# A hybrid attention block on one core: the stick-breaking scan reads its sigmoid from PSUM, and one PSUM bank moves from the transposed weights to the scores

## The chip, the cores and the metric

The kernel runs on one core of a Trainium2 chip. The metric is the device time of one execution in microseconds (us). Before the change the median of three runs is 3167.59 us (3167.34 to 3170.79).

## What is computed

The program is one layer of a streaming encoder on 2048 positions of width 1024, all in float32: a projection of the normalised input into the queries, keys and values of two attention groups (differential attention with 4 heads, stick-breaking attention with 8 heads), an output projection, a feed-forward part, and a last normalisation. The change lies in the stick-breaking group:

```
def stick_breaking(q, k, v, norm_g):
    # beta = sigmoid(q.k/sqrt(d)); A[t,s] = beta[t,s] * prod_{s<j<t} (1 - beta[t,j]), s < t
    ...
        z = jnp.einsum('bqhd,bkhd->bhqk', qb, kb) * scale
        ...
        suffix = lax.cumsum(neg_log_1m_beta, axis=3, reverse=True)
        log_a = jax.nn.log_sigmoid(z) - (suffix - neg_log_1m_beta)
        a = jnp.where(mask, jnp.exp(log_a), 0.0)
        outs.append(jnp.einsum('bhqk,bkhd->bqhd', a, v[:, :t1].astype(jnp.float32)))
```

The weight of a key is its beta times the product of (1 - beta) of all later keys. The kernel forms that product with a scan that runs backwards along the keys, with 1 - beta = sigmoid(-z).

## The kernel before

The sequence is cut into four tiles of 512 positions (T = 0 to 3). A tile has eight units g: 0 to 3 are the differential heads, 4 to 7 hold two stick-breaking heads each. The first half of the program (up to about 1500 us) is attention. Beside the attention of one unit, the projection of the next one (`project`, three matmuls of fp32r halves, lines 314 to 316) is issued in small pieces, and in the last unit the output projection of tile 0. The order is a written-out list of steps: `scores_of` of a stage is issued up to `LA_S = 3` stages ahead of `weigh_of`, and a scheduler with priorities then fixes the queue of each engine when the program is built. Which PSUM bank a tile gets is fixed there too.

PSUM has eight banks: two for projections (pool `ps_p`), two for scores (`ps_s`, `PSS = 2`), three for transposed things (`ps_t`, `PST = 3`), one for outputs (`ps_o`). A stick-breaking stage is a pair j of query blocks, a head m and a chunk c of 512 keys. For each of its two query blocks, here called a row of work:

- TensorE (PE) writes the scores to a bank of `ps_s` (lines 668, 669, on the diagonal also 671).
- ScalarE (ACT) reads them twice: sigmoid(-z) to the tile half `om` (line 830) and sigmoid(z) to `be` (831). Both lie in the SBUF tile `row`. Behind them it copies one carried column (836).
- VectorE (DVE) scans `om` backwards in place (834). Both data operands of this instruction are the same SBUF tile.
- GpSimd (POOL) multiplies `be` by the shifted `om` (837, on the diagonal 839).

`weigh` then takes up to four 128x128 blocks: PE transposes them into a bank of `ps_t` (691, tile `ps_at`), ACT copies them to SBUF (696 for head m = 0, 700 otherwise), for m = 0 DVE also forms the rest `al` (697, it reads the same bank), and two or three groups later PE multiplies by the values (715 and 716, or 723). The differential heads use the same two pools: DVE reads their scores (777), ACT takes the exponential (782), and their transposed weights go through 691 and 700.

`transpose_v` (line 644) uses `ps_t` too: the values of the next unit are transposed into a bank (649, tile `ps_vt`), which ACT (655, 656, or 651) and DVE (657) empty as soon as a slot of the value pool is free.

Of the kernel before, what the change touches and what calls it, by code (L numbers as in the profile page):

```python
# [13 lines left out]
AF = mybir.ActivationFunctionType  # L14
ALU = mybir.AluOpType
# [47 lines left out]
FIN = 6  # L63
KB = 5
VB = 5
PSS = 2
PST = 3
PSO = 1
PSP = 2
ROWB = 5  # L70
# [27 lines left out]
def hybrid_block(ctx, tc, xT, n1g, w_in, lq1, lk1, lq2, lk2, subg, sbg, w_out, n2g, w_up, w_down, fg, outT):  # L98
    nc = tc.nc
    PE, V, A, G = nc.tensor, nc.vector, nc.scalar, nc.gpsimd  # L100
# [217 lines left out]
    def blk(d):  # L318
        return slice(d * P, (d + 1) * P)
# [4 lines left out]
    def defer(fn, steps):  # L324
        later.append([steps, fn])
# [98 lines left out]
    with ExitStack() as pa:  # L424
# [6 lines left out]
        ap_ = pa.enter_context(tc.tile_pool(name="ap", bufs=2))  # L431
        ps_s = pa.enter_context(tc.tile_pool(name="ps_s", bufs=PSS, space=PSUM))
        ps_t = pa.enter_context(tc.tile_pool(name="ps_t", bufs=PST, space=PSUM))
        ps_o = pa.enter_context(tc.tile_pool(name="ps_o", bufs=PSO, space=PSUM))
# [228 lines left out]
        def scores(T, g, m, qb, c, n, diag):  # L663

            kv = kt[T, g, c]
            q2, ql = q2t[T, g], qlt[T, g]
            ps = ps_s.tile([P, TW], F32, tag="ps", name="ps_sc")
            PE.matmul(ps[:, :n], lhsT=q2[:, m, blk(qb)], rhs=kv[:, m * TW:m * TW + n], start=True, stop=False)  # L668
            PE.matmul(ps[:, :n], lhsT=ql[:, m, blk(qb)], rhs=kv[:, m * TW:m * TW + n], start=False, stop=not diag)  # L669
            if diag:  # L670
                PE.matmul(ps[:, n - P:n], lhsT=identb, rhs=maskb, start=False, stop=True)
            return ps
# [62 lines left out]
        def finish(T, g, j, po):  # L735

            ot = ap_.tile([P, 2 * P], F32, tag="ot", name="ot")
            A.copy(ot, po)
            nc.sync.dma_start(o_scr[T][g][:, j * 256:(j + 1) * 256], ot)
            sq = ap_.tile([P, 2 * P], F32, tag="osq", name="osq", bufs=1)  # L740
            A.activation(out=sq, in_=ot, func=AF.Square, scale=lam_inv8 if g < NDIFF else 0.125)
            nh, h0 = (1, g) if g < NDIFF else (2, 4 + 2 * (g - 4))
            out = mean_sq[T % 2].rearrange("p (h b) -> p b h", h=NHEADS)[:, 2 * j:2 * j + 2, h0:h0 + nh]
            V.reduce_sum(out=out, in_=sq.rearrange("p (b h c) -> p b h c", h=nh, c=P // nh), axis=mybir.AxisListType.X)
            if g == NG - 1 and j == 1:
                head_rms(T)

        def next_po():
            return ps_o.tile([P, 2 * P], F32, tag="po", name="po")
# [61 lines left out]
        def sb_stages(T, g):  # L811
            out = []
            state = {}

            def stage(j, m, c):
                last_kb = 4 * T + 2 * j + 1
                mine = {}

                def scores_of():
                    row = rowp.tile([P, 2052], F32, tag="row", name="row")  # L820
                    tv = row.rearrange("p (q k c) -> p q k c", q=2, k=2)
                    prev = state.get((j, m))
                    state[j, m] = tv
                    mine["tv"] = tv
                    for qq in range(2):
                        qb = 2 * j + qq
                        n = TW if c < T else (qb + 1) * P
                        ps = scores(T, g, m, qb, c, n, c == T)
                        be, om = tv[:, qq, 0, :], tv[:, qq, 1, :]
                        A.activation(out=om[:, :n], in_=ps[:, :n], func=AF.Sigmoid, scale=-1.0)  # L830
                        A.activation(out=be[:, :n], in_=ps[:, :n], func=AF.Sigmoid)
                        rev = om[:, :n][:, ::-1]
                        init = 1.0 if c == T else prev[:, qq, 1, 0:1]
                        V.tensor_tensor_scan(out=rev, data0=rev, data1=rev, initial=init, op0=ALU.mult, op1=ALU.bypass)  # L834
                        if c < T:
                            A.copy(om[:, n:n + 1], prev[:, qq, 1, 0:1])
                            G.tensor_tensor(out=be[:, :n], in0=be[:, :n], in1=om[:, 1:n + 1], op=ALU.mult)  # L837
                        else:
                            G.tensor_tensor(out=be[:, :n - 1], in0=be[:, :n - 1], in1=om[:, 1:n], op=ALU.mult)
                        yield  # L840

                def weigh_of():
                    tv = mine["tv"]
                    hi_kb = last_kb if c == T else 4 * c + 3

                    def done():
                        if c > 0:
                            return
                        if m == 1:
                            finish(T, g, j, state[j, 1, "po"]["po"])  # L850
                            return

                        oq = ap_.tile([P, 2 * P], F32, tag="oq", name="oq")
                        A.copy(oq, mine_po["po"])  # L854
                        po = state.setdefault((j, 1, "po"), {})

                        def join():
                            if "po" not in po:
                                po["po"] = next_po()
                            for qq in range(2):  # L860
                                PE.matmul(po["po"][:, qq * P:qq * P + 64], lhsT=oq[:, blk(qq)], rhs=fold,
                                          start="open" not in po, stop=False)
                                po["open"] = True

                        def late_join():
                            if "fold" in po:
                                po.pop("fold")()

                        po["fold"] = join
                        defer(late_join, FIN)  # L870

                    mine_po = state.setdefault((j, m, "po"), {})
                    yield from weigh(T, g, mine_po, list(range(4 * c, hi_kb + 1)),
                                     lambda qq, kb: tv[:, qq, 0, blk(kb - 4 * c)], False, m, last_kb, c == T, c == 0, done)

                return scores_of, weigh_of, 2, 2 * (j + 1) if c == T else 4

            return [stage(j, m, c) for j in range(2) for m in range(2) for c in range(T, -1, -1)]
# [317 lines left out]
```

## Time and profile before

| | |
|---|---|
| median of 3 runs | 3167.59 us |
| the profiled execution | 3167.63 us |
| its span in the trace | 3165.6 us |
| mean granted clock of TensorE | 0.981 |
| PE busy | 3002.9 us (95%) |
| DVE busy | 1806.9 us (57%) |
| ACT busy | 1230.7 us (39%) |
| POOL busy | 1054.8 us (33%) |

The span is the time between the first and the last instruction of the trace; the execution is 2.0 us longer. Busy time is the union of an engine's instructions. The ends of matmuls are modelled, so short gaps of PE can be larger than they look. [...]

### The profile page before, as it was taken

What the parts mean: (1) busy time and instruction counts of PE and PEld (TensorE: products, weight loads), DVE (VectorE), ACT (ScalarE), POOL (GpSimd) and SP (SyncE); (2) the same over time, 40 slices, a digit from 0 to 9 for tenths busy, and PEclk for the clock granted to TensorE, in tenths of its full rate; (3) what the DMA queues carried; (4) which work ended last, traced back from release to release, by engine and by line L of the source; (5) the groups of instructions that cost most, each with busy time, mean ns of one, the idle gap of its engine ahead of it and who ended that gap; (6) DMA issues with size and microseconds to landing.
All of it is one profiled execution on the core that took longest, in us unless ns stands there. A gap on an engine that the chain in (4) does not pass through costs nothing.

```text
span 3165.6 us, 42061 instructions
## 1 busy us (share of the span) xinstructions
PE 3002.9 (95%) x15562; PEld 2512.8 (79%) x15562; DVE 1806.9 (57%) x2841; ACT 1230.7 (39%) x2414; POOL 1054.8 (33%) x733
## 2 busy tenths in 40 slices
PE   7888999999989999988988999999999999999997
PEld 5677887888878888877776888888887788888886
DVE  5465567665777767889545444444446544444445
ACT  5344566645766547767333111111113111111113
POOL 3353034202453003556333323332235333333234
PEclk9999999999999999999999999999999999999998
DMA  7777655555443543331666111111114311111111
GB/s 250 253 242 237 210 186 186 162 168 174 137 150 111 154 135 111 114 101 32 212 204 204 48 46 54 47 53 47 40 54 137 103 53 54 47 47 52 42 47 54
DMA packets 153277, 376.73 MB, mean 119 GB/s; under 512 B 20336, under 2 KB 35184, under 8 KB 153072
## 3 DMA queue, kind: packets, MB, share of 16 engines
q1 hardware_dynamic: 153072, 374.04, 37.0%
q8 instruction: 123, 2.02, 0.3%
q14 instruction: 82, 0.67, 0.1%
HBM read 261.24 MB, written 70.78 MB: 105 GB/s over the span
## 4 chain that ended last, share of the span: by engine, by line
PE 45%; DVE 2%; DMA 2%; issue 1%; ACT 1%; POOL 0%; SPq 0%; DVEq 0%; POOLq 0%; ACTq 0%
PE ps_d L314 7%; PE ps_u L315 7%; PE ps_d L315 7%; PE ps_u L316 7%; PE ps_d L316 7%; PE ps_u L314 7%; DMA om<-os 1%; PE ps_h L314 1%; PE ps_h L316 1%; PE ps_h L315 1%; DMA xr<-in_xT 1%; POOL sqs L1035 0%; DVE acc L1056 0%; DVE sqs L394 0%; DMA hraw<-hs 0%
## 5 line engine op out<-in xcount | busy, mean ns | idle before, releaser
L834 DVE TENSOR_TENSOR_SCAN row<-row 128x512 f32<-128x512 f32 (+2 forms) x320 | 429.2, 1351 | 128.1 <-ACT row L830 109.9
L1109 DVE TENSOR_TENSOR acc<-ps_d,acc 128x512 f32<-128x512 f32 (+1 forms) x520 | 348.5, 680 | 253.4 <-PE ps_d L316 252.7
L314 PE MATMUL ps_d<-uh,dh 128*128 128x512 f32 (+1 forms) x1040 | 403.2, 388 | 2.6 <-DVE acc L1109 2.6
L315 PE MATMUL ps_d<-ul,dh 128*128 128x512 f32 (+1 forms) x1040 | 402.8, 387 | 0.0
L316 PE MATMUL ps_d<-uh,dl 128*128 128x512 f32 (+1 forms) x1040 | 402.3, 387 | 0.0
L254 POOL TENSOR_TENSOR wl<-wr,wh 128x1024 fp32r<-128x1024 f32 x119 | 289.6, 2434 | 249.1 <-ACT wh L230 221.1
L314 PE MATMUL ps_proj<-xh,wh 128*128 128x512 f32 x768 | 334.7, 436 | 10.0 <-ACT xh L530 6.9
L837 POOL TENSOR_TENSOR row<-row 128x512 f32<-128x512 f32 x192 | 248.4, 1301 | 255.8 <-DVE row L834 156.9
L254 POOL TENSOR_TENSOR dl<-wr,dh 128x1024 fp32r<-128x1024 f32 x64 | 152.0, 2395 | 542.0 <-ACT dh L230 542.0
L315 PE MATMUL ps_proj<-xl,wh 128*128 128x512 f32 x768 | 309.7, 403 | 14.4 <-POOL xl L525 12.9
L316 PE MATMUL ps_proj<-xh,wl 128*128 128x512 f32 x768 | 310.0, 404 | 9.4 <-POOL wl L254 8.8
L723 PEld LDWEIGHTS po<-v,at 128*128 128x128 f32 x2176 | 286.3, 194 | 28.7 <-ACT oq L854 8.4
L723 PE MATMUL po<-v,at 128*128 128x128 f32 (+1 forms) x2176 | 293.9, 276 | 6.4 <-ACT oq L854 5.1
L691 PE MATMUL ps_at<-ident,row 128*128 128x128 f32 x1632 | 259.1, 276 | 27.6 <-DVE al L697 20.1
L1096 DVE TENSOR_TENSOR ul<-u,uh 128x512 fp32r<-128x512 f32 x128 | 179.1, 1399 | 180.1 <-ACT uh L1095 180.0
L230 ACT CAST dh<-wr 128x1024 fp32r<-128x1024 f32 x64 | 64.1, 1049 | 553.1 <-PE ps_d L315 553.1
L668 PE MATMUL ps_sc<-k,q 128*128 128x512 f32 (+3 forms) x640 | 257.9, 404 | 19.8 <-DMA q<-pjh 10.3
L1092 POOL TENSOR_TENSOR u<-u 128x512 f32<-128x512 f32 x128 | 134.4, 1050 | 395.2 <-DVE u L1091 381.2
L1091 DVE SCALAR_TENSOR_TENSOR u<-ps_u,rb 128x512 f32<-128x512 f32 x128 | 88.4, 691 | 300.4 <-PE ps_u L316 300.4
L691 PEld LDWEIGHTS ps_at<-ident,row 128*128 128x128 f32 x1632 | 197.7, 144 | 63.9 <-issue 14.9
L1095 ACT CAST uh<-u 128x512 fp32r<-128x512 f32 x128 | 79.7, 622 | 414.6 <-POOL u L1092 414.6
L669 PE MATMUL ps_sc<-k,qlow 128*128 128x512 f32 (+3 forms) x640 | 234.1, 367 | 0.0
(184 smaller groups left out, 6307.0 us busy)
## 6 DMA issues: line engine op xcount, KB each, us to landing
wh<-ws SPq DMA_DIRECT2D x72, 512.0 KB, 3.6
wl<-ws SPq DMA_DIRECT2D x72, 512.0 KB, 4.4
wr<-in_w_up SPq DMA_DIRECT2D x64, 512.0 KB, 3.7
wr<-in_w_down SPq DMA_DIRECT2D x64, 512.0 KB, 3.5
k<-ks SPq DMA_DIRECT2D x48, 512.0 KB, 4.3
q<-pjh SPq DMA_DIRECT2D x128, 128.0 KB, 3.1
wr<-in_w_out SPq DMA_DIRECT2D x32, 512.0 KB, 4.9
ws<-wh SPq DMA_DIRECT2D x24, 512.0 KB, 5.0
```

The costliest lines, as they stand in the source:

```text
L254: G.tensor_tensor(out=wl, in0=wr, in1=f32(wh), op=ALU.subtract)
L314: PE.matmul(ps, lhsT=wh[:, cs], rhs=xh, start=start, stop=False)
L315: PE.matmul(ps, lhsT=wh[:, cs], rhs=xl, start=False, stop=False)
L316: PE.matmul(ps, lhsT=wl[:, cs], rhs=xh, start=False, stop=stop)
L668: PE.matmul(ps[:, :n], lhsT=q2[:, m, blk(qb)], rhs=kv[:, m * TW:m * TW + n], start=True, stop=False)
L669: PE.matmul(ps[:, :n], lhsT=ql[:, m, blk(qb)], rhs=kv[:, m * TW:m * TW + n], start=False, stop=not diag)
L691: PE.transpose(pt[:, o:o + P], getter(qq, kb), ident)
L723: PE.matmul(po["po"][:, qq * P + c0:(qq + 1) * P], lhsT=f32(at)[:, so + n * P:so + (n + 1) * P], rhs=vv, start="open" not in po, stop=ends ...
L834: V.tensor_tensor_scan(out=rev, data0=rev, data1=rev, initial=init, op0=ALU.mult, op1=ALU.bypass)
L837: G.tensor_tensor(out=be[:, :n], in0=be[:, :n], in1=om[:, 1:n + 1], op=ALU.mult)
L1096: V.tensor_tensor(out=ul, in0=u, in1=f32(uh), op=ALU.subtract)
L1109: V.tensor_tensor(out=a, in0=ps[:, cs], in1=a, op=ALU.add)
```

## The change

`PSS` and `PST` change places in size: three score banks, two for transposed things. In a stick-breaking row the two sigmoids change their order: sigmoid(z) to `be` comes first, then sigmoid(-z) is written over the scores in their own PSUM bank. The scan reads its first operand from that bank, its second operand, which `bypass` ignores, is `be` in SBUF, and it writes `om` in SBUF as before.

```
-PSS = 2
-PST = 3
+PSS = 3
+PST = 2
...
                         be, om = tv[:, qq, 0, :], tv[:, qq, 1, :]
-                        A.activation(out=om[:, :n], in_=ps[:, :n], func=AF.Sigmoid, scale=-1.0)
                         A.activation(out=be[:, :n], in_=ps[:, :n], func=AF.Sigmoid)
-                        rev = om[:, :n][:, ::-1]
+                        A.activation(out=ps[:, :n], in_=ps[:, :n], func=AF.Sigmoid, scale=-1.0)
+                        rev, src = om[:, :n][:, ::-1], ps[:, :n][:, ::-1]
                         init = 1.0 if c == T else prev[:, qq, 1, 0:1]
-                        V.tensor_tensor_scan(out=rev, data0=rev, data1=rev, initial=init, op0=ALU.mult, op1=ALU.bypass)
+                        V.tensor_tensor_scan(out=rev, data0=src, data1=be[:, :n], initial=init, op0=ALU.mult, op1=ALU.bypass)
```

The change also moves instructions, since the queues are made when the program is built. Two places show it, both in tile T = 3, in a stretch of head m = 0. Numbers are those of the built program; `row_13761` and `row_13804` are the `row` tiles of two stages that follow each other, each with two scans, and the scan (line 834) is printed as SCALAR_TENSOR_TENSOR.

The queue of DVE, before:

```order
L697 TENSOR_TENSOR al_13758<-ps_at_13752,at_13757 128x512
L834 SCALAR_TENSOR_TENSOR row_13761<-row_13761,row_13711 128x512
L697 TENSOR_TENSOR al_13780<-ps_at_13774,at_13779 128x512
L834 SCALAR_TENSOR_TENSOR row_13761<-row_13761,row_13711 128x512
L697 TENSOR_TENSOR al_13801<-ps_at_13795,at_13800 128x512
L834 SCALAR_TENSOR_TENSOR row_13804<-row_13804,row_13761 128x512
```

and with the change:

```order
L834 SCALAR_TENSOR_TENSOR row_13761<-ps_sc_13762,row_13711,row_13761 128x512
L697 TENSOR_TENSOR al_13758<-ps_at_13752,at_13757 128x512
L834 SCALAR_TENSOR_TENSOR row_13761<-ps_sc_13783,row_13711,row_13761 128x512
L834 SCALAR_TENSOR_TENSOR row_13804<-ps_sc_13805,row_13761,row_13804 128x512
L697 TENSOR_TENSOR al_13780<-ps_at_13774,at_13779 128x512
L834 SCALAR_TENSOR_TENSOR row_13804<-ps_sc_13826,row_13761,row_13804 128x512
```

The scans have moved ahead of the rests `al`: the scan of `row_13804` stood behind `al_13801`, and now stands in front of `al_13780`.

The queue of PE at the same place, before (`ps_at` are transposed weights, `ps_sc` scores):

```order
L715 MATMUL po_13747<-at_13678,v_12290 128x128
L716 MATMUL po_13747<-al_13679,v_12290 128x128
L691 MATMUL ps_at_13774<-ident_63,row_13612 128x128 x4
L668 MATMUL ps_sc_13783<-k_12292,q2_12310 128x512
L669 MATMUL ps_sc_13783<-k_12292,qlow1_300 128x512
L715 MATMUL po_13747<-at_13707,v_12294 128x256
L716 MATMUL po_13747<-al_13708,v_12294 128x256
```

and around the same group of transposes with the change:

```order
L668 MATMUL ps_sc_13826<-k_12298,q2_12310 128x512
L669 MATMUL ps_sc_13826<-k_12298,qlow1_300 128x512
L691 MATMUL ps_at_13774<-ident_63,row_13612 128x128 x4
L715 MATMUL po_13747<-at_13757,v_12300 128x256
L716 MATMUL po_13747<-al_13758,v_12300 128x256
```

The scores stand further ahead of the transposes (`ps_sc_13826`, two rows later than `ps_sc_13783`, is now in front of `ps_at_13774`), and the products behind them take the group just before (`at_13757`) where they took one three groups back (`at_13707`).

Up to the next group of transposes, with the change:

```order
L314 MATMUL ps_proj_13918<-xh0_9470,wh_13507 128x512
L715 MATMUL po_13747<-at_13779,v_12300 128x256
L315 MATMUL ps_proj_13918<-xl0_9471,wh_13507 128x512
L668 MATMUL ps_sc_13864<-k_12304,q2_12310 128x512
L669 MATMUL ps_sc_13864<-k_12304,qlow1_300 128x512
L316 MATMUL ps_proj_13918<-xh0_9470,wl_13508 128x512
L691 MATMUL ps_at_13795<-ident_63,row_13659 128x128 x4
```

Three matmuls of a projection have come in between `ps_at_13774` and `ps_at_13795`; before, none stood there. In both programs the tile of transposed values `ps_vt_13694` has its bank of `ps_t` throughout these rows: it is written some rows earlier and read for the last time some rows later.

## Rows read from the trace of the kernel before

**Rows 1.** The page: busy time of each engine (us, share of the span, instructions).

```profile
PE 3002.9 (95%) x15562; PEld 2512.8 (79%) x15562; DVE 1806.9 (57%) x2841; ACT 1230.7 (39%) x2414; POOL 1054.8 (33%) x733
```

**Rows 2.** By stretch: PE, PEld, DVE, ACT, POOL busy, granted clock, DMA share, GB/s.

```profile
800.00:900.00 100.00, 96.71 (x638) 84.87 (x637) 71.16 (x73) 69.91 (x177) 45.59 (x46) 0.98 0.46 139
900.00:1000.00 100.00, 89.94 (x569) 76.87 (x568) 75.77 (x74) 68.24 (x163) 53.10 (x46) 0.93 0.45 138
...
1100.00:1200.00 100.00, 99.34 (x612) 85.21 (x611) 67.50 (x181) 53.16 (x77) 0.00 (x0) 1.00 0.42 136
1200.00:1300.00 100.00, 93.54 (x637) 81.67 (x636) 73.65 (x81) 71.95 (x174) 47.82 (x39) 1.00 0.37 112
1300.00:1400.00 100.00, 92.37 (x603) 80.44 (x603) 77.17 (x73) 69.57 (x175) 52.46 (x45) 0.98 0.34 99
1400.00:1500.00 100.00, 87.75 (x644) 77.62 (x644) 92.58 (x89) 78.15 (x191) 69.59 (x46) 1.00 0.17 52
```

**Rows 3.** Groups by line and shape: line engine op | busy us, mean ns | idle before.

```profile
L834 DVE TENSOR_TENSOR_SCAN row<-row 128x512 f32<-128x512 f32 x224 | 339.0, 1522 | 87.4 <-ACT row L830 69.9 <-POOL row L839 8.1 <-POOL row L837 5.2
L1096 DVE TENSOR_TENSOR ul<-u,uh 128x512 fp32r<-128x512 f32 x128 | 179.1, 1399 | 180.1 <-ACT uh L1095 180.0
L697 DVE TENSOR_TENSOR al<-ps_at,at 128x512 fp32r<-128x512 f32 x112 | 75.3, 673 | 22.8 <-ACT at L696 22.2
L697 DVE TENSOR_TENSOR al<-ps_at,at 128x384 fp32r<-128x384 f32 x32 | 17.2, 536 | 13.4 <-ACT at L696 13.4
```

**Rows 4.** The same view: ACT, POOL and the waits of PE.

```profile
L831 ACT ACTIVATE row<-ps_sc 128x512 f32<-128x512 f32 x224 | 137.6, 614 | 0.0
L831 ACT ACTIVATE row<-ps_sc 128x128 f32<-128x128 f32 x32 | 9.3, 290 | 0.0
L837 POOL TENSOR_TENSOR row<-row 128x512 f32<-128x512 f32 x192 | 248.4, 1301 | 255.8 <-DVE row L834 156.9 <-ACT row L831 27.1 <-ACT row L830 18.0
L525 POOL TENSOR_TENSOR xl<-xraw,xh 128x512 fp32r<-128x512 f32 x24 | 36.9, 1565 | 1.5 <-ACT xh L524 1.5
L315 PE MATMUL ps_proj<-xl,wh 128*128 128x512 f32 x768 | 309.7, 403 | 14.4 <-POOL xl L525 12.9 <-DVE xl L531 1.4
```

**Rows 5.** Instructions in order of time, DVE and POOL, head m = 0 in tile 3.

```profile
1339.90 0.87 POOL L839 TENSOR_TENSOR row<-row 128x383 f32<-128x383 f32 x1 [0.99 <-DVE row L834]
1340.56 1.28 DVE L834 TENSOR_TENSOR_SCAN row<-row 128x512 f32<-128x512 f32 x1
1344.33 1.10 POOL L837 TENSOR_TENSOR row<-row 128x512 f32<-128x512 f32 x1 [1.25 <-DVE row L834]
1344.67 1.84 DVE L834 TENSOR_TENSOR_SCAN row<-row 128x512 f32<-128x512 f32 x1
```

**Rows 6.** The same stretch: PE's transposes and scores, ACT's sigmoid and copy.

```profile
1340.37 0.66 PE L691 MATMUL ps_at<-ident,row 128*128 128x128 f32 x4 [0.46 <-DVE al L697]
1340.78 0.48 PE L668 MATMUL ps_sc<-k,q 128*128 128x512 f32 x1
1341.06 0.59 ACT L696 CAST at<-ps_at 128x512 fp32r<-128x512 f32 x1 [0.27 <-PE ps_at L691]
1341.55 0.60 ACT L830 ACTIVATE row<-ps_sc 128x512 f32<-128x512 f32 x1
1342.03 0.60 ACT L831 ACTIVATE row<-ps_sc 128x512 f32<-128x512 f32 x1
1342.58 0.63 PE L691 MATMUL ps_at<-ident,row 128*128 128x128 f32 x4 [0.61 <-DVE al L697]
1344.80 0.66 PE L691 MATMUL ps_at<-ident,row 128*128 128x128 f32 x4 [0.65 <-DVE al L697]
1347.23 0.63 PE L691 MATMUL ps_at<-ident,row 128*128 128x128 f32 x4 [0.83 <-DVE al L697]
```

**Rows 7.** One tile of transposed values in the same view: its first writer, its last reader.

```profile
1334.53 0.60 PE L649 MATMUL ps_vt<-ident,pj 128*128 128x128 f32 x4
1369.68 0.41 DVE L657 TENSOR_TENSOR v<-ps_vt,v 128x256 fp32r<-128x256 f32 x1
```

## The prediction

> **What bounds the kernel now.** I read the page first: TensorE is busy 95% of the span, no other engine above 57% [rows 1]. So only time in which PE idles can be won, and the next view, busy time by stretch, says where it idles [rows 2]. In 1000 to 1200 us, the differential heads of tile 3, PE is 98 to 99% busy. In the stick-breaking heads it is not: 96.7 and 89.9 us of each 100 in 800 to 1000 (end of tile 2 and the change to tile 3), and 93.5, 92.4 and 87.8 in 1200 to 1500. That is 13.4 us idle in the first pair and 26.3 in the last three, 39.7 in all. In 1400 to 1500 DVE is busy 92.6 us, more than PE. The instructions in order of time tell what PE waits for: four groups of transposes start at 1340.37, 1342.58, 1344.80 and 1347.23, each the moment DVE has formed a rest `al` [rows 6]. The row of work takes (1347.23 - 1340.37) / 3 = 2.29 us, and PE idles 0.61 to 0.83 of it, about 0.70.
>
> **Why DVE is slow there.** A scan of 512 columns takes 1.28 us where POOL's product has ended early in it, and 1.84 where a product runs beside it; the mean of 224 is 1.52 [rows 3, 5]. The group view gives the pattern. Line 1096, two SBUF inputs, means 1399 ns; line 697, the same shape with one input in PSUM and one in SBUF, 673, although POOL is busy 46 to 70 us of each 100 where it runs [rows 2, 3]. The scan now has two SBUF operands, and afterwards one in PSUM and one in SBUF, so it joins line 697.
>
> **The change, part by part.** Durations are from the profiled execution, 3167.63 us (span 3165.6 and 2.0 outside); the median of the runs is 3167.59, the same.
>
> *The scan.* 224 scans fall from 1.52 to 1.28 us: 224 x 0.24 = 54 us of DVE. The 96 shorter ones are priced at the same share, some 14 us, so 68 in all. On the path lies only what PE now waits. With the scan at 1.28 and the rest at 0.67, DVE needs 1.95 us for a row of head m = 0 in place of 2.29 [rows 3, 5, 6]. The 0.34 won is half of PE's 0.70. So I take half of the 26.3 us in 1200 to 1500: 13 us. In 800 to 1000, part of the idle time belongs to the change of tile, so a third: 4.5 us. Bounds: nothing (PE finds its next wait at once), and all 39.7. No row shows a scan that reads PSUM. From below it costs nothing more. From above I take the whole fixed part of the nearest row that reads PSUM, line 697: (673 - 536) / 128 = 1.07 ns a column, so 673 - 512 x 1.07 = 125 ns are fixed [rows 3], and 320 x 0.125 = 40 us of DVE would go, more than half of the 68. I add nothing, since only a part of those 125 ns can be PSUM's.
>
> [...]
>
> *POOL.* Its product means 1.30 us and takes 1.10 where nothing holds it [rows 4, 5]: 192 x 0.2 = 38 us of POOL, all beside other work (POOL is busy 33%). But the low halves of the next tile's input, line 525, have the same shape and mean 1.57, and PE waited 12.9 us for them [rows 4]. They stand between such products and scans; I take 4 of the 12.9 (0 to 9).
>
> *ACT.* Same two sigmoids. The scan must now wait for the second: 0.48 us later, by the starts 1341.55 and 1342.03 [rows 6]. In the steady row that is hidden by DVE's queue: the scan that starts at 1344.67 uses the sigmoid of 1341.55 [rows 5, 6]. Priced at nothing; without that cover each of 320 rows would start up to 0.48 late, which POOL's product and then the transposes would feel only if the rows ahead run out. The second sigmoid now writes the bank it reads. No row shows ACT doing so. From below nothing, since PE's accumulating matmuls add to a bank at no extra time (line 315 means 403 ns [rows 4]). From above, its part per column doubles: (614 - 290) / 384 = 0.84 ns, or 432 ns on 512 columns, 97 us on 224 rows. I take nothing, the nearer row. [...]
>
> *Three score banks.* A bank is now held from the scores to the end of the scan: 1340.78 to 1344.67 + 1.84 = 1346.51, 5.7 us [rows 5, 6]. Three banks carry a row each 1.9 us, just under the 1.95 that DVE needs, and less once the scan is shorter. Priced at nothing. If it goes wrong, PE stands at line 668 until a scan ends.
>
> *Two banks for transposed things.* This is the cost. Transposed values wait in one of these banks until a value slot is free: the tile written at 1334.53 is last read at 1370.09, 35.6 us [rows 7]. Counted in the order of the changed program, 15 such tiles, from the second unit of tile 2 on, hold their bank while some 180 of the 432 groups of transposed weights pass. Those groups had two banks; now they have one, and each must be emptied before the next is transposed. For a third of them (head m = 0) that is transposes 0.66, copy 0.59 and rest 0.67, with handovers about 2.0 us, if ACT and DVE are free [rows 3, 6]. That is under 2.29: no loss. If a scan stands right ahead of the rest, it is 1.28 more, 3.3 us, 1.0 lost. So 60 groups cost 0 to 60 us. The scan mostly runs beside the transposes and the copy (1.25 us together), so I take 0.1 us each, 6 us. For the other 120 the chain is 1.25 us, and a wait comes only from ACT's queue, up to 1 us each when something long stands there: 0 to 120. PE has other work between two groups, as the order with projections in between shows, so I take 0.04 each, 5 us. In 1000 to 1200, where PE is full, that is a loss in whole.
>
> **Sum.** 13 + 4.5 + 4 - 6 - 5 = 10.5 us. 3167.6 - 10.5 = 3157.
>
> **The rivals.**
>
> *The single bank decides (slower).* In place of the wait for DVE, PE waits for the one bank left beside the values. It decides from the point where the rest `al` of a group stands behind a whole scan: the order of the change puts scans ahead of rests, which speaks for it, as does PE's 98 to 99% in 1000 to 1200 [rows 2]. Against it: a faster scan shortens that very wait. Price: 60 x 0.6 + 120 x 0.1 = 48 us lost against 21.5 won: 3194. Chance 0.24.
>
> *Sigmoid in place is slow (slower).* With 0.43 us more per row, ACT, now 70 to 78% busy in 1200 to 1500, has 128 rows there (4 units of 32) and would need 55 us more of the 80 it has free. It would be at its limit; I price half of the 97 us above, less the gain of 21: 3195. Chance 0.06.
>
> *It cancels (same).* The gain on DVE is given back at the banks, 15 us each way: 3161 to 3174. For it: PE is the bound almost everywhere. Chance 0.24. The case that the scan is not relieved at all, because its output or its ignored operand still meets POOL, belongs here with a small loss; line 697 speaks against it.
>
> *All of it is won.* If the waits for DVE vanish and the banks cost nothing, 30 to 40 us: 3132. Against it: half of PE's idle time in a row remains PE's own chain. Chance 0.06.
>
> **How the numbers follow.** The forecast, 3157, has 0.40. About 0.2%, 6.3 us, is what a measurement of this kernel can tell from no change. Faster by more than that: 0.40 + 0.06 = 0.46; the same: 0.24; slower: 0.24 + 0.06 = 0.30. The forecast's own range is 3140 to 3161. The range that should hold the time 8 times in 10 reaches from 3128 (all of the idle time won) to 3195 (the prices of the two slow rivals). Beyond it stay the upper halves of these two and a sliver below.
>
> **What would show it.** Right: the mean of the 512-column scan near 1.28 us and of POOL's product near 1.10; DVE well below 92 us in the last full 100 us of the stick-breaking heads; PE's waits for line 697 shorter there. Wrong at the banks: PE's waits at line 691 for line 697, 700 or 657 grow, and PE falls under 98% in the differential heads of tile 3. Wrong at ACT: line 831 well above 614 ns. Wrong at the scores: PE waits at line 668 for line 834. The forecast is wrong if PE's idle time in 1200 to 1500 does not fall, or if what it loses there comes back in 600 to 800 and 1000 to 1200.

## The result and the profile after

The change makes the kernel faster. The median is 3136.93 us (3134.95 to 3137.71). The kernel before, run beside it, took 3167.34, 3167.59 and 3170.79 us; a fourth execution of it took 12711.88 us, for a reason that nothing here shows, and is left out. The ratio is 0.9899, with a 95% interval of 0.988 to 0.9919, so the gain is some 31 to 32 us where 10.5 were forecast. The time lies inside the forecast's wide range (3128 to 3195) and below the forecast's own range (3140 to 3161).

| | before | after |
|---|---|---|
| the profiled execution | 3167.63 us | 3137.71 us |
| its span | 3165.6 us | 3135.6 us |
| mean granted clock of TensorE | 0.981 | 0.983 |
| PE busy | 3002.9 us | 3003.9 us |
| DVE busy | 1806.9 us | 1723.2 us |
| POOL busy | 1054.8 us | 1000.0 us |

PE does the same work in the same time, so all of the 30 us between the two spans is time in which PE no longer idles. The page of the changed kernel, the line that answers to [rows 1]:

```profile
PE 3003.9 (96%) x15562; PEld 2509.3 (80%) x15562; DVE 1723.2 (55%) x2841; ACT 1238.4 (39%) x2414; POOL 1000.0 (32%) x733
```

Where it went is read first from the finish of each unit. Line 738 is the copy with which ACT takes a finished output out of its bank; the row gives its duration (min, median, max, in ns), then the starts of the first and the last one in us. Before:

```profile
L738 ACT COPY ot<-po x64: 347/373/414, 70.4 to 1509.4; 128x256 f32<-128x256 f32 x64
```

and after:

```profile
L738 ACT COPY ot<-po x64: 349/373/432, 72.5 to 1479.4; 128x256 f32<-128x256 f32 x64
```

The last unit of attention ends 30.0 us earlier: the whole gain lies in the attention half, none in the feed-forward part behind it. In the same way the last unit of tile 2 ends at 1030.0 in place of 1041.7, so 11.7 us are won up to there and 18.3 in tile 3.

Busy time by stretch of the changed kernel, in the columns of [rows 2] (PE, PEld, DVE, ACT, POOL, granted clock, DMA share, GB/s):

```profile
800.00:900.00 100.00, 99.01 (x660) 85.97 (x659) 64.37 (x73) 74.01 (x181) 44.01 (x46) 1.00 0.44 137
900.00:1000.00 100.00, 94.28 (x607) 79.72 (x606) 68.35 (x81) 71.41 (x170) 50.75 (x47) 0.98 0.49 151
...
1100.00:1200.00 100.00, 98.38 (x628) 85.41 (x628) 64.14 (x171) 54.68 (x82) 0.41 (x1) 1.00 0.44 142
1200.00:1300.00 100.00, 99.13 (x659) 85.78 (x657) 68.53 (x79) 77.79 (x191) 44.63 (x45) 1.00 0.32 102
1300.00:1400.00 100.00, 97.47 (x648) 83.31 (x646) 74.70 (x82) 78.34 (x190) 53.73 (x50) 1.00 0.40 123
1400.00:1500.00 100.00, 93.37 (x624) 80.84 (x624) 71.58 (x94) 68.86 (x159) 45.74 (x39) 0.98 0.22 70
```

In 1200 to 1500 us PE idles 10.0 us in place of 26.3, in 800 to 1000 it idles 6.7 in place of 13.4 [rows 2]. In 1100 to 1200 PE idles 1.0 us more. DVE is busy 71.6 us in 1400 to 1500 where it was 92.6.

The work in a stretch is not the same in both, since tile 3 begins some 12 us earlier and its attention ends at 1479.8 in place of 1509.8. The same view from the end of tile 2's attention to the end of tile 3's compares equal work. Before:

```profile
1041.70:1509.80 468.10, 440.31 (x2912) 383.56 (x2912) 351.68 (x539) 307.27 (x662) 172.26 (x131) 1.00 0.35 107
```

and after:

```profile
1030.00:1479.80 449.80, 441.69 (x2912) 381.73 (x2912) 313.39 (x537) 310.41 (x662) 137.38 (x131) 1.00 0.35 110
```

PE idles 8.1 us of it where it idled 27.8. In the last 100 us before the end of the attention DVE is busy 77.3 us, and 86.0 before.

The groups that answer to [rows 3, 4], in the changed kernel:

```profile
L834 DVE TENSOR_TENSOR_SCAN row<-ps_sc,row 128x512 f32<-128x512 f32 x224 | 282.9, 1271 | 134.3 <-ACT ps_sc L831 114.7 <-PE ps_at L691 8.2 <-issue 4.0
L837 POOL TENSOR_TENSOR row<-row 128x512 f32<-128x512 f32 x192 | 211.8, 1104 | 259.4 <-DVE row L834 229.1 <-ACT ps_sc L831 7.9 <-ACT at L696 7.2
L831 ACT ACTIVATE ps_sc<-ps_sc 128x512 f32<-128x512 f32 x224 | 135.7, 606 | 0.0
L525 POOL TENSOR_TENSOR xl<-xraw,xh 128x512 fp32r<-128x512 f32 x24 | 33.9, 1435 | 2.8 <-ACT xh L524 2.8
L315 PE MATMUL ps_proj<-xl,wh 128*128 128x512 f32 x768 | 310.9, 405 | 8.8 <-POOL xl L525 6.7 <-DVE xl L531 2.1
```

The scan falls from 1522 to 1271 ns and POOL's product from 1301 to 1104. The sigmoid written over its own scores takes 606 ns against 614 [rows 4]: nothing is paid for it.

What PE waited for, before (groups of PE by line, shapes taken together):

```profile
L691 PE MATMUL ps_at<-ident,row 128*128 128x128 f32 x1632 | 259.1, 276 | 27.6 <-DVE al L697 20.1 <-POOL row L837 3.0 <-DVE v L657 3.0
L668 PE MATMUL ps_sc<-k,q 128*128 128x512 f32 (+3 forms) x640 | 257.9, 404 | 19.8 <-DMA q<-pjh 10.3 <-DVE mn L777 3.9 <-ACT row L831 2.3
L723 PE MATMUL po<-v,at 128*128 128x128 f32 (+1 forms) x2176 | 293.9, 276 | 6.4 <-ACT oq L854 5.1 <-ACT ot L738 0.9
L715 PE MATMUL po<-at,v 128*128 128x256 f32 (+1 forms) x288 | 77.8, 291 | 5.9 <-ACT ot L738 5.9
```

and after:

```profile
L691 PE MATMUL ps_at<-ident,row 128*128 128x128 f32 x1632 | 255.2, 275 | 6.5 <-DVE al L697 2.5 <-DVE row L792 1.5 <-DVE v L657 1.0
L668 PE MATMUL ps_sc<-k,q 128*128 128x512 f32 (+3 forms) x640 | 254.4, 400 | 24.1 <-DMA q<-pjh 9.0 <-DVE row L834 7.2 <-DMA k<-pjh 3.2
L723 PE MATMUL po<-v,at 128*128 128x128 f32 (+1 forms) x2176 | 291.5, 274 | 1.7 <-ACT ot L738 1.6
L715 PE MATMUL po<-at,v 128*128 128x256 f32 (+1 forms) x288 | 78.4, 292 | 0.6 <-ACT ot L738 0.6
```

The idle time ahead of PE's matmuls, added over all of its groups, falls from 154.8 to 124.0 us, by 30.8. The transposes (691) give 21.1 of it, the products with the values (715, 723) 10.0, the low halves of the input (line 315, [rows 4]) 5.6; the scores (668) take back 4.3, since they now wait 7.2 us for scans to end; the other lines together take back 1.6.

The steady row shows what replaced the pattern of [rows 5, 6]. Instructions in order of time, head m = 0 of tile 3 in the changed kernel:

```profile
1325.68 0.67 DVE L697 TENSOR_TENSOR al<-ps_at,at 128x512 fp32r<-128x512 f32 x1
...
1326.26 2.45 DVE L834 TENSOR_TENSOR_SCAN row<-ps_sc,row 128x512 f32<-128x512 f32 x2
...
1326.40 0.66 PE L691 MATMUL ps_at<-ident,row 128*128 128x128 f32 x4
...
1327.68 2.29 POOL L837 TENSOR_TENSOR row<-row 128x512 f32<-128x512 f32 x2 [0.65 <-ACT at L696]
...
1328.62 0.67 DVE L697 TENSOR_TENSOR al<-ps_at,at 128x512 fp32r<-128x512 f32 x1
...
1329.57 0.60 PE L691 MATMUL ps_at<-ident,row 128*128 128x128 f32 x4
```

Two scans stand back to back in 2.45 us, although POOL's two products run beside them from 1327.68 on. PE's transposes carry no idle time in brackets, where each of those in [rows 6] has 0.46 to 0.83 us. The group of 1329.57 follows a rest `al` that began at 1328.62: DVE ends in time.

### The profile page after: what moved, and what is told of

It reads as the page before. It is cut to its first block, busy times and chain, and to the rows that moved or that the text cites. A ratio compares the mean times of both kernels' runs of the same rounds, so it can differ in the third digit from the quotient of the medians.

```text
span 3135.6 us, 41864 instructions
## 1 busy us (share of the span) xinstructions
PE 3003.9 (96%) x15562; PEld 2509.3 (80%) x15562; DVE 1723.2 (55%) x2841; ACT 1238.4 (39%) x2414; POOL 1000.0 (32%) x733
## 4 chain that ended last, share of the span: by engine, by line
PE 46%; DVE 2%; DMA 1%; issue 1%; ACT 1%; POOL 0%; SPq 0%; DVEq 0%; POOLq 0%; ACTq 0%
PE ps_u L315 7%; PE ps_u L316 7%; PE ps_u L314 7%; PE ps_d L314 7%; PE ps_d L315 7%; PE ps_d L316 7%; DMA om<-os 1%; PE ps_h L316 1%; PE ps_h L314 1%; PE ps_h L315 1%; DMA xr<-in_xT 0%; POOL sqs L1035 0%; DVE acc L1056 0%; DVE dgh L216 0%; PE ps_om L359 0%
## 5 line engine op out<-in xcount | busy, mean ns | idle before, releaser
L834 DVE TENSOR_TENSOR_SCAN row<-ps_sc,row 128x512 f32<-128x512 f32 (+2 forms) x320 | 347.2, 1095 | 178.0 <-ACT ps_sc L831 157.3
L837 POOL TENSOR_TENSOR row<-row 128x512 f32<-128x512 f32 x192 | 211.8, 1104 | 259.4 <-DVE row L834 229.1
```

Source lines behind the costliest of these rows:

```text
L834: V.tensor_tensor_scan(out=rev, data0=src, data1=be[:, :n], initial=init, op0=ALU.mult, op1=ALU.bypass)
```

## The experiments

Two theories stood against each other at the start. By the first, the gain is the home of the scan's operand: with one input in PSUM the scan and POOL's product stop holding each other up. By the second, the banks matter as much, as a cost (one bank left beside the waiting values) or as a part of the gain (three score banks let PE run ahead). The sizes of the two pools and the scan were therefore separated, and then the scan's two changes from each other.

### The banks alone

```
-PSS = 2
-PST = 3
+PSS = 3
+PST = 2
```

> The kernel before with three score banks and two for transposed things, the scan as it was (both operands in SBUF). Theory (the operand's home does it, the banks cost a little): the mean of the 512-column scan stays at 1.5 us, DVE stays the bound in the last stretch, time 3167 to 3185. Rival (the third score bank does it, by more look-ahead): 3137 to 3150 with the scan still at 1.5 us.

Measured: 3189.0 us (3184.45 to 3193.63) against 3170.27, a ratio of 1.0056 (1.0041 to 1.0072): 18 us lost. The groups of this run:

```profile
L834 DVE TENSOR_TENSOR_SCAN row<-row 128x512 f32<-128x512 f32 x224 | 337.9, 1518 | 98.9 <-ACT row L830 77.9 <-issue 8.9 <-POOL row L839 7.8
L691 PE MATMUL ps_at<-ident,row 128*128 128x128 f32 x1632 | 258.5, 278 | 35.7 <-DVE al L697 28.6 <-DVE v L657 2.2 <-DVE row L792 1.8
```

The time lies 4 us above the range that was expected. The scan keeps its 1.52 us, and PE's waits at the transposes for the rest `al` grow from 20.1 to 28.6 us. So moving the bank costs about 18 us beside the slow scan. That the single bank left at the transposes is what costs fits, but is not shown alone: 6.1 of the 8.5 us more stand while a tile of transposed values holds a bank (15 such tiles in the trace, as the prediction counted), 2.5 at other times, and the third score bank of the same run also changes the order of the queues. Not all of the cost is idle time: of the 23.6 us by which the profiled span is longer (3189.2 against 3165.6), PE's busy time has 12.2 (3015.1 against 3002.9), at a mean granted clock of 0.977 against 0.981.

### The scan alone

The scan and the sigmoids of the change, with the old `PSS = 2` and `PST = 3`.

> The changed scan and order of the sigmoids, but two score banks and three for transposed things. Theory: the scan's mean falls to 1.27 us as in the change, but a score bank is held to the scan's end, some 5 us, and two of them pass a row each 2.5 us: PE waits at line 668 for line 834, some 60 us in all, and the time is 3150 to 3200. Rival (the banks are all of it): 3169 or more although nothing waits at line 668. If two score banks are enough: 3125 to 3137, since the third bank of transposed things comes back.

Measured: 3137.9 us (3135.03 to 3141.33), a ratio of 0.9896 (0.9883 to 0.991). The span is 3135.7 us, that of the whole change is 3135.6.

```profile
L834 DVE TENSOR_TENSOR_SCAN row<-ps_sc,row 128x512 f32<-128x512 f32 x224 | 284.1, 1272 | 139.4 <-ACT ps_sc L831 127.2 <-ACT row L836 6.7 <-POOL row L837 2.2
L691 PE MATMUL ps_at<-ident,row 128*128 128x128 f32 x1632 | 255.9, 274 | 0.9 <-DVE al L697 0.7 <-ACT at L700 0.2
L668 PE MATMUL ps_sc<-k,q 128*128 128x512 f32 x448 | 199.0, 444 | 17.8 <-DVE row L834 14.1 <-DVE mn L777 1.8
```

The expected 60 us of waits at line 668 did not come (18.6 us there end with a scan, over all shapes), and the time lies 12 us under the range that went with them, 1 us above the range for the case that two score banks are enough. All of the gain is here, without any change of the banks. Beside the fast scan the bank that moves is worth nothing in either direction: with it at the transposes PE waits 0.9 us there and 17.8 us at the 512-column scores, mostly for scans to end; with it at the scores 6.5 and 7.4. The two trade places, and the longer waits at the scores cost nothing in the sum. The effects do not add: 18 lost and 32 won, alone, would leave 14, and together they give 32. The cost of the moved bank is there only beside the slow scan.

### Only the operand that nobody uses

Banks as in the change, but both sigmoids as before: the scan still reads `om` from SBUF and writes over it. Only its second operand, which `bypass` ignores, points to the scores in PSUM.

```
-V.tensor_tensor_scan(out=rev, data0=rev, data1=rev, initial=init, op0=ALU.mult, op1=ALU.bypass)
+V.tensor_tensor_scan(out=rev, data0=rev, data1=ps[:, :n], initial=init, op0=ALU.mult, op1=ALU.bypass)
```

> Banks as in the change, the order of the sigmoids and their target (SBUF) as before; of the scan only the second operand, which bypass ignores, is moved: it points to the score bank in PSUM. Theory (one SBUF operand is what frees the scan): the mean of the 512-column scan is 1.27 to 1.30 us and the time 3130 to 3145, like the change. Rival (the sigmoid written in place, or the scan's data coming from PSUM, does it): scan at 1.5 us and 3165 or more.

Measured: 3136.64 us (3135.99 to 3137.99), a ratio of 0.9892 (0.9879 to 0.9906).

```profile
L834 DVE TENSOR_TENSOR_SCAN row<-row,ps_sc 128x512 f32<-128x512 f32 x224 | 282.1, 1267 | 133.1 <-ACT row L831 112.2 <-PE ps_at L691 10.1 <-issue 4.0
L837 POOL TENSOR_TENSOR row<-row 128x512 f32<-128x512 f32 x192 | 211.7, 1103 | 257.7 <-DVE row L834 214.0 <-PE ps_sc L669 13.5 <-ACT at L696 8.0
```

The same scan, product and time as with the whole change. From the run with the banks alone this one differs in that operand only, and takes 52 us less (3136.64 against 3189.0, on the same chip). What the sigmoid writes, and that the scan's data lie in PSUM, plays no part. It is enough here that one of the two operands is not in SBUF, even the one whose values are never used: 1267 ns against 1518 with the banks alone.

### Another SBUF tile as the ignored operand

The control: the kernel before, with the ignored operand in a different SBUF tile.

```
-V.tensor_tensor_scan(out=rev, data0=rev, data1=rev, initial=init, op0=ALU.mult, op1=ALU.bypass)
+V.tensor_tensor_scan(out=rev, data0=rev, data1=base[:, :n], initial=init, op0=ALU.mult, op1=ALU.bypass)
```

> The kernel before, old banks; of the scan only the second, ignored operand is changed, to another tile in SBUF (a constant). Theory: still two SBUF operands, so the scan stays at 1.5 us and the time at 3163 to 3175. Rival (reading the same tile twice is what costs): scan at 1.28 us, time 3130 to 3145.

Measured: 3170.87 us against 3170.24, a ratio of 0.9997 (0.9987 to 1.0007).

```profile
L834 DVE TENSOR_TENSOR_SCAN row<-row,base 128x512 f32<-128x512 f32 x224 | 339.8, 1525 | 87.0 <-ACT row L830 69.3 <-POOL row L839 8.0 <-POOL row L837 5.2
L837 POOL TENSOR_TENSOR row<-row 128x512 f32<-128x512 f32 x192 | 247.7, 1297 | 255.8 <-DVE row L834 155.9 <-ACT row L831 28.5 <-ACT row L830 18.1
```

Not that the two operands were the same tile, nor that the second was written over while it was read, made the scan slow: a foreign tile in SBUF costs the same 1.52 us.

### Without POOL's product

```
-G.tensor_tensor(out=be[:, :n], in0=be[:, :n], in1=om[:, 1:n + 1], op=ALU.mult)
...
-G.tensor_tensor(out=be[:, :n - 1], in0=be[:, :n - 1], in1=om[:, 1:n], op=ALU.mult)
```

> The kernel before without POOL's product of beta and the shifted scan (lines 837 and 839 are left out, so the weights are beta alone); the scan is as before, both operands in SBUF, old banks. Theory (POOL's product is what holds the scan up): the mean of the 512-column scan falls to 1.27 to 1.32 us though nothing of it was changed, the time to 3130 to 3150. Rival (two SBUF operands, or a scan in place, are slow by themselves): scan at 1.5 us, time 3150 or more.

Measured: 3120.79 us (3115.99 to 3125.83), a ratio of 0.9846 (0.983 to 0.9861), some 9 us faster than expected.

```profile
L834 DVE TENSOR_TENSOR_SCAN row<-row 128x512 f32<-128x512 f32 x224 | 288.3, 1295 | 99.2 <-ACT row L830 98.7
```

Here the scan still has both operands in SBUF, and without the product beside it falls from 1522 to 1295 ns. So it is the meeting of the two that costs, not the two operands by themselves. What is left above 1271 ns comes from few scans, as the durations of all 320 show (min, median, max), first in this run and then in the changed kernel:

```profile
L834 DVE TENSOR_TENSOR_SCAN row<-row x320: 392/1274/3099, 157.7 to 1443.0; 128x512 f32<-128x512 f32 x96, 128x128 f32<-128x128 f32 x32, 128x384 f32<-128x384 f32 x32
L834 DVE TENSOR_TENSOR_SCAN row<-ps_sc,row x320: 398/1274/1287, 162.2 to 1464.4; 128x512 f32<-128x512 f32 x96, 128x128 f32<-128x128 f32 x32, 128x384 f32<-128x384 f32 x32
```

The medians are equal. The long ones are scans that still met other work of POOL: six of 512 columns spend more than half of their time beside it and take 2.11 us on average. With POOL's product gone the kernel also loses a link of each row's chain, so its 49 us are not a bound for this change alone.

### A sixth slot for the values

To test whether the held bank still costs something, the changed kernel was run with a sixth slot in the value pool, into which the transposed values can leave their bank earlier.

```
-VB = 5
+VB = 6
```

> The change with six value slots in place of five. In the built order the transposed values then leave their bank at once in tile 2 (2 or 3 groups of weights pass in place of 9 to 13) and some groups earlier in tile 3. If the one bank left beside them costs: tile 2 gets faster by some 5 us, PE's waits at line 691 fall, time 3125 to 3133. If it costs nothing: 3134 to 3140.

Measured: 3131.44 us (3129.26 to 3134.47), a ratio of 0.9876 (0.9862 to 0.9889). On the same chip the kernel with only the ignored operand moved, which has five slots, took 3136.64 (3135.99 to 3137.99); the ranges do not meet, so some 5 us are won. Most of them lie in tile 2, as expected: its attention takes 395.0 us in place of 400.1. But PE's waits at the transposes fall only from 6.5 (in the change) to 5.3 us, so the wait for the bank does not give them. Two more runs asked whether the same slot helps with the old banks too. First the scan of the change with old banks and six slots:

> Scan and sigmoids of the change, two score banks and three for transposed things, and six value slots. If the early release of the transposed values' bank is what the sixth slot gave, it gives less here, where a second bank was left anyway: 3133 to 3140. If the slot helps for another reason (values that arrive earlier): 3127 to 3133, as much as with the change's banks.

Measured: 3132.84 us (3128.93 to 3139.86), a ratio of 0.9881 (0.9864 to 0.9898). Then the smallest edit, the kernel before with six slots and the ignored operand in PSUM:

> The kernel before with two edits: the scan's ignored operand points to the score bank, and six value slots; old banks, old order of the sigmoids, sigmoid(-z) in SBUF. Theory (the operand is all of the gain): scan at 1.27 us and 3125 to 3140. Rival (the change's other parts were needed with two score banks): 3145 or more, with PE waiting at line 668.

Measured: 3131.97 us (3129.54 to 3137.48), a ratio of 0.9878 (0.9864 to 0.9893), with a scan of 1269 ns. All three come out within 2 us of each other, with either number of banks. With the change's banks the slot's 5 us are clear. With the old banks they are likely but not shown: 3128.93 to 3139.86 with the slot and 3135.03 to 3141.33 without (the scan alone, on another chip) overlap, though tile 2 takes 399.0 us with it in both runs and 402.4 without. The smallest edit was not run with five slots. Through which wait the slot helps stays open. These are the fastest versions that compute the whole block, and the last one reaches them with one operand and one constant changed.

## Why the prediction was right, and where its size was wrong

**Right: the mechanism.** The scan was to fall to 1.28 us and measures 1271 ns; the product to 1.10 and measures 1104. DVE's busy time falls by 83.7 us where the sum priced the scans at 68. Counted over the traces, the scans of 512 columns that run beside POOL for more than half of their time take 1641 ns before (46 of them) and 1270 after (82); those with no POOL beside them take 1274 (80) and 1268 (96). The experiments agree: with POOL's product beside it the scan takes 1525 ns with a second SBUF tile as its ignored operand and 1267 with that operand in PSUM, and without the product 1295 with both in SBUF.

**Right: the signs.** DVE is busy 71.6 us in 1400 to 1500 where it was 92.6 [rows 2], and less too when equal work is compared (77.3 and 86.0), PE's idle time in 1200 to 1500 fell, and ACT's line 831 did not rise above 614 ns. The later order of the sigmoids is hidden as far as PE's waits tell: DVE stood 157.3 us ahead of its scans for line 831, where it had stood 109.9 for line 830 before, but PE's waits for POOL's product at the transposes, 3.0 us before, are gone. No run that keeps POOL's product has the fast scan without a wait for line 831 (with only the ignored operand moved it still waits 112.2 us for it at 512 columns), so the price of the order was not separated.

**Right: in-place and PSUM reading at nothing.** The rival of a slow in-place sigmoid, with its bound of 97 us, falls with 606 ns. The nearer row held. That PE adds to a bank at no extra time stands in the trace before: at 512 columns the matmul that begins a score bank (668) means 440 ns, the one that adds to it (669) 396. The bound of 40 us for a PSUM read falls as well: the median scan takes 1274 ns with its data in PSUM and the ignored operand in SBUF, and 1274 with both in SBUF and no product beside it.

**Wrong: the part of PE's idle time that the scan wins.** The step that failed is "So I take half of the 26.3 us in 1200 to 1500: 13 us", with the third of 13.4 for 800 to 1000. It assumed that PE would find the rest of the row's chain still in its way and that only 0.34 of about 0.70 us could be won. Measured, 16.3 of the 26.3 and 6.7 of the 13.4 went, and that is already net of what the banks cost. In tile 3 as a whole the idle time at the transposes fell from 19.4 to 1.7 us, so nearly all of it was won and not half. In the steady row of the changed kernel the transposes have no idle time at all. The built order, shown ahead of the prediction, had put scans ahead; the sum still priced each row as if it kept the order of before. How much of the step is the shorter scan and how much the moved order was not separated.

By what PE waited for, the miss of some 21 us has two halves. At the transposes and the scores together 16.8 us were won (21.1 less 4.3), where the sum has 6.5 (17.5 less 11 for the banks). Another 10.0 were won behind ACT, which the sum does not name.

**Wrong: the price of the banks.** The sum subtracts 6 and 5 us for the single bank. With the banks alone 18 us are lost, more than the sum says; beside the fast scan nothing that the comparison of 3135.6 with 3135.7 can show. The third score bank, priced at nothing, came with 7.2 us of waits for scans at line 668, fewer than the 18.6 with two. The terms were added as if independent, and the runs show that they are not. It fits that PE's waits for the rest `al`, which had grown to 28.6 us with the banks alone, are 2.5 us in the change: the bank is held until DVE comes to the rest, and a faster scan lets it come sooner. The rival "The single bank decides" named just that ("a faster scan shortens that very wait") as what spoke against it. The run with the banks alone fits its mechanism but not its 48 us, and in the change it does not decide.

**Not in the sum: waits behind ACT.** PE's waits at 715 and 723 fell from 12.3 to 2.3 us. They end with copies by ACT (738, 854). ACT stood 100.9 us at line 836 before, waiting for scans, and 42.1 after:

```profile
L836 ACT COPY row<-row 128x1 f32<-128x1 f32 x192 | 39.5, 206 | 101.2 <-DVE row L834 100.9
L836 ACT COPY row<-row 128x1 f32<-128x1 f32 x192 | 37.3, 195 | 43.8 <-DVE row L834 42.1 <-POOL row L837 1.2
```

The longest of these waits, before, in order of time:

```profile
931.88 0.19 ACT L836 COPY row<-row 128x1 f32<-128x1 f32 x1 [4.36 <-DVE row L834]
931.97 0.37 ACT L738 COPY ot<-po 128x256 f32<-128x256 f32 x1
...
932.39 0.58 PE L715 MATMUL po<-at,v 128*128 128x256 f32 x1 [3.77 <-ACT ot L738]
```

The copy that PE needs stands behind line 836 on ACT's queue, which stands behind a scan. The same order is ahead of eight waits of more than 0.2 us between 795 and 1395 us, 10.5 us in all, and none of the eight is left in the changed kernel. At 715 and 723 together the run with the scan alone has 2.0 us of waits, that with only the ignored operand moved 2.3 and that with the banks alone 17.4, so it is the faster scan, with the order built for it, that took them away. Nearly all of them lie in the stretches whose 39.7 us the prediction divided, but its working priced only the wait for the rest `al`.

**About right: the input.** PE's waits for line 525 were to fall by 4 us of 12.9; they fell by 6.2, to 6.7, with the instruction at 1435 ns in place of 1565.

So the nearest of the cases was "All of it is won" (3132, at a chance of 0.06), 5 us from the result, where the forecast is 20 us from it. What the prediction held against that case, "half of PE's idle time in a row remains PE's own chain", is the failed step again. That the time lies in the wide range owes as much to its width, 67 us, as to the sum.

## What to carry to other kernels

Look at where an instruction's operands lie even when the operation ignores one of them: pointing the ignored operand of a VectorE scan to PSUM gave here the whole gain of a larger change (3136.64 us against 3136.93). Follow the slow engine's delay through every queue that waits for it, not through the longest chain alone: here about half of what was missed stood behind a copy of one column (10.0 of some 21 us). When a change takes time from the engine that another's buffers wait for, price the buffers with the engine's new time and in the new order, not with the old waits: here the cost of a bank and that of the engine that empties it did not add (18 us lost and 32 won alone, 32 won together). And test the parts alone, for a part that was neutral in the sum here (the banks) was a loss of 18 us by itself.

## What was not expected of the hardware

- The operand that `bypass` ignores counts: the same scan takes 1525 ns with that operand in another SBUF tile and 1267 ns with it in PSUM, with POOL's product beside it.
- An ACT sigmoid of 512 columns that overwrites the PSUM bank it reads takes 606 ns, no more than one that writes to SBUF (608 ns for line 830 in the same run).
- The granted clock of TensorE averages 0.93 before and 0.98 after in 900 to 1000 us, where PE was busy 89.9 and 94.3 us [rows 2]. Before, it was 0.50 in 935 to 945 us, with PE's wait of 3.77 us, shown above, just ahead, and 1.00 in the 5 us behind. In 1400 to 1500, where PE idled 12 us in waits of at most 1.64, it averages 1.00 [rows 2]. The view by stretch, before:

```profile
930.00:935.00 5.00, 2.61 (x8) 2.32 (x9) 5.00 (x5) 2.43 (x8) 2.79 (x3) 0.64 0.87 210
935.00:940.00 5.00, 2.45 (x6) 1.34 (x5) 4.25 (x4) 2.18 (x5) 3.77 (x3) 0.50 0.82 255
940.00:945.00 5.00, 3.56 (x8) 2.63 (x9) 0.00 (x0) 0.00 (x0) 5.00 (x5) 0.50 0.35 123
945.00:950.00 5.00, 4.40 (x31) 3.58 (x30) 2.77 (x4) 3.29 (x9) 0.73 (x2) 1.00 0.10 38
```
